# Layer 0's linear attention: its inputs asked for behind the attention keys, state sums one cycle ahead, gate and norm in one step, output weights split in its second pass

## The chip, the cores and the metric

The kernel runs on one core of one Trainium2 chip. The metric is the time of one execution on the device in microseconds (us), the median of several. Five engines work side by side, each through its own queue in order: TensorE (PE: matmuls, with a separate row PEld for the loading of weights), VectorE (DVE), ScalarE (ACT), GpSimd (POOL) and SyncE (SP), whose queue here only issues DMAs. They wait for one another by semaphores.

## What is computed

Two layers over 2048 latent tokens and 256 context tokens, in float32. Layer 0 mixes two branches side by side, a softmax attention over eight heads and a gated linear attention (GLA) over four heads, and a projection with the weight `w_out` joins them. The change lies in layer 0 alone. Its linear part, cut to what matters:

```python
def step(state, inp):
    qi, ki, vi, gi = inp
    b = jnp.cumsum(gi, axis=-2)
    b_last = b[..., -1:, :]
    q_t = qi * jnp.exp(b)
    k_t = ki * jnp.exp(-b)
    att = jnp.where(mask, jnp.einsum('bhld,bhmd->bhlm', q_t, k_t), 0.0)
    o = jnp.einsum('bhld,bhde->bhle', q_t, state) + jnp.einsum('bhlm,bhme->bhle', att, vi)
    k_dec = ki * jnp.exp(b_last - b)
    state = state * jnp.exp(b_last)[..., 0, :, None] + jnp.einsum('bhld,bhle->bhde', k_dec, vi)
    return state, o
...
a = a.reshape(bsz, n, A_WIDTH) * jax.nn.silu(za)
b = rms_norm(b, gla_gain).reshape(bsz, n, B_WIDTH).astype(zb.dtype) * jax.nn.silu(zb)
return jnp.dot(jnp.concatenate([a, b], axis=-1), w_out)
```

The scan runs once forward and once backward over the tokens, and the two outputs are added.

## The kernel before

Tokens are cut into 18 tiles of 128 (two of context, sixteen latent). Layer 0 runs in stages: `even_latent` and `even_rest` make queries, keys, values and gates and leave them in HBM; `even_mix` runs the softmax attention with the linear attention woven into it, and then the projection.

**The softmax attention** (`even_attention`, L961) takes four pairs of heads (j), and for each pair five blocks of queries (nb: one of 256 context queries over two key tiles, four of 512 over all 18 key tiles). For a key tile, PE makes scores in ten matmuls (L1121), ACT takes the exponential into a buffer `apt` (seven of them), and DVE adds it to a running sum `acc` (L1128). The products with the values (L1032, the "tails") are held back: when six key tiles are pending, `flush` does four tails in a row. A finished block is ended by `end` and `finish` (L948 to L958): matmuls that sum the denominators over partitions, then ACT, DVE and POOL, and a store. `flush` does the ends that are due ahead of the tails.

**The linear attention** (`gla`, L679) is a Python generator, `side`. It yields the name of a slot that it wants ("before", "after", "middle", "turn", "second", "unit"), and `place` runs its next piece when the attention comes to a slot of that name: "before", "turn", "unit" and "second" lie in a flush ahead of its tails, "after" behind its tails, "middle" between two flushes, when four key tiles are pending. `issue_after` puts the piece's instructions behind the named ones on the same engine, and the attention's next matmul behind the piece's last one. So PE's order is written out by hand: what a piece waits for, the whole of PE waits for. The order of the other queues comes from the tile scheduler, by the order in the program and by readiness in its own model.

In its first pass, one cycle takes two flushes. For token tile c: `decays(c)` makes the decay factors (`mid` and `hs`, matmuls L762 and L766), the scaled queries `gqt` and keys `gkt` (ACT Exp, then DVE L776; one buffer each); behind the same flush's tails `values(c - 1)` multiplies the scores of the tile before with the values (L817), copies them out (L819), and multiplies `gkt` of the tile before with the values (L823, state sums, scaled into `D` by L824); `scan` then carries the forward state on POOL. The next flush turns queries and keys (`turn`), `within` makes the scores. PSUM gives the linear attention, the turns and the denominators two banks in all (tag "gl").

In its second pass, a slot "second" for each tile, in the backward order: `write` turns the finished tile before (L883), `carried` adds queries times state (L857, L858), `squares` sums squares on ACT and takes the power -1/2 on POOL (`rpow`, L207 to L210), `back` carries the backward state (DVE L837 and L838, POOL L839), `gated` scales by the norm on DVE (L875) and multiplies with the gate on POOL (L876). A flush that has an end due takes no "second".

Behind both passes the side splits the projection's weights: 16 units of 128x512 (`load_unit` L1228, `split_unit` L1231), each split into a high part (ACT copy) and a rest (DVE subtract, L1235), with one slot "unit" for each, into buffers that the linear attention has left. The unit 15 and the loads of the gate rows come behind the attention. `project_load` and `project_split` read and split the first tile of the result.

**The start of the stage.** `want = next(side)` at L1024 runs the head of `gla` before the attention's first loads are traced: loads of `gate_w` (97 partitions), `tri`, `halves`, `gla_norm`, and the inputs of the first tiles (`glr`, `gu`), all on SP's queue. The buffer `ge` that takes `gate_w` lies where the weights of the stage before lay, so that its load waits for that stage's last matmuls. `gw` is made from it: a copy on ACT, a DMA of its own last row, and a subtraction on DVE. Behind that head come the attention's loads (L973 for keys `akh`, `akl` and queries `aq`; L1001 for values). Each DMA takes the next of eight semaphores in turn, and waits until the DMA that had it last has landed.

## Time and profile before

| | us |
|---|---|
| median of 3 runs | 3635.44 |
| lowest and highest | 3629.82, 3636.42 |
| the profiled execution, its time | 3634.33 |
| its span, from the first to the last instruction | 3632.5 |
| PE busy in the span | 3489.4 |
| DVE, ACT, POOL busy | 2346.1, 1391.7, 1344.5 |
| mean granted TensorE clock | 0.985 |

In the rows of the trace a line gives the start, the duration, the engine (SPq is a DMA issue on SP's queue), the line of the kernel, the operation and "out<-in" by the program's names; in brackets stands how long the engine was idle before it, and what ended that. A table of stretches gives the busy time of each engine, the instructions in it in brackets, the granted clock of PE (1.00 is full speed), the busy share of the 16 DMA engines, and GB/s. A row of waits gives the waiting engine and line, what it waited for, and the sum, the number and the longest of these waits. A row of groups gives busy time and mean duration in ns, and behind the bar the idle time before the group's instructions.

### The profile page before, as it was taken

How to read it: one execution, taken by the hardware profiler on the slowest of the kernel's cores; microseconds unless marked ns; L12 is line 12 of the kernel's file. 1: busy time of each engine (PE TensorE's matmuls, PEld its weight loads, DVE VectorE, ACT ScalarE, POOL GpSimd, SP SyncE). 2: the span in 40 equal slices, each digit the busy share in tenths (PEclk: the TensorE clock that was granted, in tenths of full speed). 3: DMA queues.
4: the chain of work that ended last, by engine and by line, in shares of the span. 5: the costliest groups of instructions: out<-in, count | busy, mean ns of one | idle time of the engine just before them, and what ended most of it. 6: DMA issues, size and time to landing. Idle time of an engine off the chain costs nothing. (4 is left out here: it accounts for less than half of the span.)

```text
span 3632.5 us, 53914 instructions
## 1 busy us (share of the span) xinstructions
PE 3489.4 (96%) x19604; PEld 2693.3 (74%) x19604; DVE 2346.1 (65%) x4567; ACT 1391.7 (38%) x2516; POOL 1344.5 (37%) x1430
## 2 busy tenths in 40 slices
PE   7999989999998999999999999999899999999899
PEld 6888988888884666565556888888788887555577
DVE  4677656888884777767766335555578784666732
ACT  5444552111114545445654114444422222555510
POOL 1433430100101344433321234333444443888763
PEclk9999999999999999999999999999999999999999
DMA  7555554222214242334435544555744447888672
GB/s 250 146 158 156 140 153 133 84 69 83 76 61 133 71 126 72 104 103 121 146 97 165 178 136 128 157 160 154 237 128 139 137 132 186 216 225 213 188 235 99
DMA packets 375787, 517.06 MB, mean 142 GB/s; under 512 B 33993, under 2 KB 253593, under 8 KB 369618
## 3 DMA queue, kind: packets, MB, share of 16 engines
q1 hardware_dynamic: 330754, 422.36, 40.3%
q0 software_dynamic: 22112, 63.26, 5.7%
q10 hardware_dynamic: 22656, 27.99, 2.2%
q8 instruction: 156, 2.56, 0.3%
q14 instruction: 109, 0.89, 0.1%
HBM read 334.17 MB, written 179.30 MB: 141 GB/s over the span
## 5 line engine op out<-in xcount | busy, mean ns | idle before, releaser
L661 DVE TENSOR_REDUCE mm<-mx 128x1 f32<-128x512 f32 (+1 forms) x656 | 388.6, 629 | 82.2 <-PE mx L660 75.2
L1128 DVE TENSOR_TENSOR acc<-acc,apt 128x1024 f32<-128x1024 f32 x256 | 362.9, 1417 | 85.2 <-ACT apt L106 66.7
L106 ACT ACTIVATE apt<-st 128x1024 f32<-128x1024 f32 (+1 forms) x296 | 300.3, 1015 | 237.2 <-PE st L1121 217.2
L1121 PE MATMUL st<-aq,akh 64*128 64x512 f32 x1728 | 312.2, 410 | 2.7 <-ACT apt L106 2.5
L1032 PE MATMUL av<-apt,av 128*64 128x512 f32 x1152 | 263.2, 598 | 0.0
L1603 POOL TENSOR_TENSOR oacc<-oacc,opt 128x576 f32<-128x576 f32 (+5 forms) x192 | 223.4, 1189 | 41.0 <-ACT rl L106 19.9
L660 PE MATMUL mx<-mk,mq 96*128 96x512 f32 (+1 forms) x656 | 236.0, 373 | 0.8 <-DMA mq<-QC 0.4
L1721 DVE TENSOR_TENSOR opt<-st,tab 128x64 f32<-128x64 f32 (+10 forms) x576 | 144.5, 318 | 140.6 <-PE st L1564 68.2
L1121 PE MATMUL st<-aq,akl 64*128 64x512 f32 (+1 forms) x1152 | 230.0, 392 | 0.0
L1121 PEld LDWEIGHTS st<-aq,akh 64*128 64x128 f32 x1728 | 151.0, 186 | 86.6 <-ACT apt L106 30.1
L106 ACT ACTIVATE u<-gm 128x352 f32<-128x352 f32 (+1 forms) x140 | 68.5, 497 | 368.6 <-PE gm L131 208.5
L1480 DVE CUSTOM_DVE_ANT_1 mx<-mx,mtab 128x217 f32<-128x217 f32 (+12 forms) x576 | 184.0, 338 | 38.9 <-PE mx L1474 29.8
L1032 PEld LDWEIGHTS av<-apt,av 128*64 128x64 f32 x1152 | 77.7, 137 | 139.4 <-issue 135.7
L106 ACT ACTIVATE opt<-opt 128x930 f32<-128x930 f32 (+7 forms) x129 | 104.2, 810 | 110.8 <-DVE opt L1721 104.0
L660 PEld LDWEIGHTS mx<-mk,mq 96*128 96x128 f32 x656 | 121.2, 188 | 13.5 <-DVE mm L661 1.6
L1121 PEld LDWEIGHTS st<-aq,akl 64*128 64x128 f32 (+1 forms) x1152 | 110.4, 185 | 24.4 <-DMA akl<-KC 0.3
L129 PE MATMUL gm<-w1h,hhi 128*128 128x512 f32 x288 | 116.3, 404 | 7.3 <-ACT onat L106 7.3
L106 ACT ACTIVATE x<-px,modB,modA 128x128 f32<-128x128 f32 x272 | 99.5, 468 | 61.0 <-PE px L339 49.6
L129 PE MATMUL gm<-w0h,hhi 128*128 128x512 f32 x288 | 115.4, 401 | 2.1 <-DVE hhi L351 2.1
L210 POOL TENSOR_TENSOR oss<-oss,mhalf 128x8 f32<-128x8 f32 x68 | 113.2, 1665 | 5.1
L130 PE MATMUL gm<-w1l,hhi 128*128 128x512 f32 x288 | 114.9, 399 | 0.0
L131 PE MATMUL gm<-w1h,hlo 128*128 128x512 f32 x288 | 114.2, 397 | 0.0
(505 smaller groups left out, 9782.4 us busy)
## 6 DMA issues: line engine op xcount, KB each, us to landing
q<-Q SPq DMA_DIRECT2D x48, 512.0 KB
H<-x ACTq DMA_DIRECT2D x36, 512.0 KB
adaw<-ada_w SPq DMA_DIRECT2D x64, 256.0 KB
x<-H SPq DMA_DIRECT2D x32, 512.0 KB
wraw<-w_od SPq DMA_DIRECT2D x64, 256.0 KB
K1t<-okt POOLq DMA_DIRECT2D x32, 512.0 KB, 7.5
kt<-K1t SPq DMA_DIRECT2D x32, 512.0 KB
mtab<-rpb_q SPq DMA_DIRECT2D x16, 899.0 KB
```

The source lines that it names most:

```text
L106: return self.nc.scalar.activation(out, in_, func, **kw)
L129: self.nc.tensor.matmul(out, lh(k), rh(k), start=j == 0, stop=False)
L130: self.nc.tensor.matmul(out, lh(k), rl(k), start=False, stop=False)
L131: yield self.nc.tensor.matmul(out, ll(k), rh(k), start=False, stop=j == n - 1)
L660: mm = nc.tensor.matmul(ps[:, :w], q[:A_QK, (t % 6) * P : (t % 6) * P + P], k[:A_QK, k0 : k0 + w], start=True, stop=True)
L661: nc.vector.tensor_reduce(out=m[:, t, n : n + 1], in_=ps[:, :w], axis=AX.X, op=ALU.max)
L1032: mm = nc.tensor.matmul(O[j, nb][i * 64 : i * 64 + 64, :w], V[j, kt // TT][:, kt % TT, i * 64 : i * 64 + 64], pts[:, i, :w], start=n == 0, ...
L1121: mm = nc.tensor.matmul(ps[:, o // 64, :w], k[o : o + r, kb, kq], Q[o : o + r, qb, :w], start=m == 0, stop=m == 4)
L1128: added = nc.vector.tensor_tensor(out=acc[:, :, :w], in0=a[:, :, :w], in1=pts[:, :, :w], op=ALU.add)
L1480: nc.vector.tensor_tensor_reduce(out=s, in0=s, in1=tb[:, ri : ri + rn, ci : ci + cn], scale=1.0, scalar=-3e38, op0=ALU.add, op1=ALU.max, a ...
L1603: self.psum = nc.gpsimd.tensor_tensor(out=a, in0=a, in1=pts[:, :, a0 - r0 : a1 - r0, :], op=ALU.add)
L1721: bias = nc.vector.tensor_tensor(out=pt[:, d[0], d[1]], in0=ps[:, d[0], d[1]], in1=tabs[j][i][:, ri : ri + rn, ci : ci + cn], op=ALU.add)
```

## The change

- `want = next(side)` moves from L1024 into the pair j = 0, behind all loads of keys, rests and values. The head's ACT copy into `gw` becomes a DVE copy, and `gw`'s three steps move behind `low_rank(1)`.
- `values(c - 1)` keeps the product with the scores; the state sums become `added(c)`, one cycle ahead, in the same slot: they use the keys that `decays(c)` has made in the same flush. `scan` moves with them.
- `flush` does the due ends behind the first tail instead of ahead of all tails.
- In the second pass `carried` comes ahead of `write`; POOL's part of `back` is put behind `rpow`; `gated` is four DVE instructions of 128x128 (multiply by the norm's column, then by the gate) in place of one DVE and one POOL instruction of 128x512.
- `spare(n)` at the end of each slot of the second pass loads and splits units of the output weights, 13 of them by its count; two more follow in slots "unit", then the load and the split of the projection's first tile, from j = 3, nb = 2 on (before: a load at j = 3, nb = 4 and the split at its half).

```diff
@@ -207,7 +207,7 @@
         g = self.nc.gpsimd
         g.tensor_scalar(out=out, in0=in_, scalar1=mul, scalar2=add, op0=ALU.mult, op1=ALU.add)
         shp = list(out.shape)
-        g.tensor_tensor(out=out, in0=out, in1=self.mhalf[:, : shp[1]], op=ALU.pow)
+        return g.tensor_tensor(out=out, in0=out, in1=self.mhalf[:, : shp[1]], op=ALU.pow)
     def consts(self, es):
@@ -676,7 +676,7 @@
         return list(range(NCT - 1, -1, -1)) + list(range(NT - 1, NCT - 1, -1))
-    def gla(self, gp, gs, g1, gd, pp, tag):
+    def gla(self, gp, gs, g1, gd, pp, tag, spare):
         nc = self.nc
         g = nc.gpsimd
@@ -686,9 +686,6 @@
         raw = self.tl(gs, [P, 512], "ge")
         nc.sync.dma_start(raw[:97], self.i["gate_w"])
         gw = self.tl(g1, [98, 512], "gw", F32R, bufs=1)
-        self.act(gw[:97], raw[:97])
-        nc.sync.dma_start(gw[97:98].bitcast(F32), gw[96:97].bitcast(F32))
-        nc.vector.tensor_tensor(out=gw[64:97], in0=raw[64:97], in1=gw[64:97], op=ALU.subtract)
         tri = self.tl(g1, [P, 4, P], "tri", bufs=1)
         nc.sync.dma_start(tri[:], self.i["tri"])
         ind = self.tl(gp, [P, 2], "ind")
@@ -810,19 +807,23 @@
         def values(c):
-            gv, f, _, kt = tiles.pop(c)
-            at = scores.pop(c)
+            gv, at = tiles.pop(c)[0], scores.pop(c)
             ps = bank()
             for h in range(H):
-                nc.tensor.matmul(ps[:, h * P : h * P + P], at[:, h, :], gv[:, h * P : h * P + P], start=True, stop=True)
+                self.woven = nc.tensor.matmul(ps[:, h * P : h * P + P], at[:, h, :], gv[:, h * P : h * P + P], start=True, stop=True)
             oi = self.tl(gs, [P, 512], "goi")
             nc.vector.tensor_copy(oi[:], ps[:])
             nc.sync.dma_start(self.gO[c], oi[:])
+
+        def added(c):
+
+            gv, f, _, kt = tiles[c]
             ps = bank()
             for h in range(H):
                 self.woven = nc.tensor.matmul(ps[:, h * P : h * P + P], kt[:, h * P : h * P + P], gv[:, h * P : h * P + P], start=True, stop=True)
             nc.vector.tensor_tensor(out=Dl[c][:], in0=ps[:].rearrange("p (h t) -> p h t", h=H),
                                     in1=f[:, :, 1:2].to_broadcast([P, H, P]), op=ALU.mult)
+            scan(c, slice(0, 64), g, g, "gsf")
         state = {}
@@ -865,15 +866,14 @@
             for h in range(H):
                 hs = slice(h * P, h * P + P)
                 self.act(sq[:, hs], oi[:, hs], AF.Square, accum_out=ss[:, h : h + 1])
-            self.rpow(ss[:], ss[:], 1.0 / 128, EPS)
-            rows[c] += (ss,)
+            rows[c] += (ss, self.rpow(ss[:], ss[:], 1.0 / 128, EPS))
         def gated(c):
-            _, oi, zb, ss = rows[c]
-            o3 = oi[:].rearrange("p (h t) -> p h t", h=H)
-            nc.vector.tensor_tensor(out=o3, in0=o3, in1=ss[:].unsqueeze(2).to_broadcast([P, H, P]), op=ALU.mult)
-            g.tensor_tensor(out=oi[:], in0=oi[:], in1=zb, op=ALU.mult)
+            _, oi, zb, ss, _ = rows[c]
+            for h in range(H):
+                hs = slice(h * P, h * P + P)
+                nc.vector.scalar_tensor_tensor(out=oi[:, hs], in0=oi[:, hs], scalar=ss[:, h : h + 1], in1=zb[:, hs], op0=ALU.mult, op1=ALU.mult)
         def write(c):
@@ -893,6 +893,9 @@
         yield "after"
         low_rank(0)
         low_rank(1)
+        nc.vector.tensor_copy(gw[:97], raw[:97])
+        nc.sync.dma_start(gw[97:98].bitcast(F32), gw[96:97].bitcast(F32))
+        nc.vector.tensor_tensor(out=gw[64:97], in0=raw[64:97], in1=gw[64:97], op=ALU.subtract)
         yield "after"
         logits(0)
         low_rank(2)
@@ -909,10 +912,12 @@
                 yield "before"
                 decays(c)
                 softplus(c + 1)
+            yield "after"
             if c:
-                yield "after"
                 values(c - 1)
-                scan(c - 1, slice(0, 64), g, g, "gsf")
+            if c < NT:
+                added(c)
+            if c:
                 inputs(c + 1)
             if c < NT:
                 yield "turn"
@@ -927,16 +932,19 @@
         reads(order[0])
         for n in range(NT + 1):
             yield "second"
+            if n < NT:
+                carried(order[n])
             if n:
                 write(order[n - 1])
             if n < NT:
-                carried(order[n])
                 if n + 1 < NT:
                     reads(order[n + 1])
                 squares(order[n])
                 if n + 1 < NT:
-                    back(order[n + 1])
+                    with self.tc.issue_after(rows[order[n]][4].ins):
+                        back(order[n + 1])
                 gated(order[n])
+            spare(n)
     def finish(self, av, dacc, zt, dst, w, ap, pp, tag, lnp=None, bufs=(1, 2), out=None):
@@ -958,7 +966,7 @@
         (out or nc.sync).dma_start(dst, rc[:, :w])
         return rc
-    def even_attention(self, ap, pp, ahead, side):
+    def even_attention(self, ap, pp, side):
         nc = self.nc
         blocks = [(0, CTX, [0, 1])] + [(CTX + 512 * b, 512, list(range(NT))) for b in range(4)]
@@ -1021,7 +1029,7 @@
             return q, last
         pend, late, O, sums = [], [], {}, {}
-        want = next(side)
+        want = None
         def tail(j, nb, n, kt, pts):
@@ -1063,15 +1071,15 @@
             with ExitStack() as es:
                 for x in marks:
                     es.enter_context(self.tc.issue_after(x.ins))
-                for x in due:
-                    with self.tc.issue_after(mm.ins):
-                        mm = end(*x[1:])
-                    late.remove(x)
                 short = None
                 for n in range(5):
-                    if n == 4 and not (short and short[1] not in sums):
-                        break
-                    if not pend:
+                    if n == 1 or not pend:
+                        for x in due:
+                            with self.tc.issue_after(mm.ins):
+                                mm = end(*x[1:])
+                            late.remove(x)
+                        due = []
+                    if not pend or n == 4 and not (short and short[1] not in sums):
                         break
                     p = pend.pop(0)
                     with self.tc.issue_after(mm.ins):
@@ -1097,6 +1105,7 @@
                     next(g)
                 for p in (1, 2):
                     load(keys(0, p), low(0, p), values(0, p))
+                want = next(side)
             else:
                 load(low(j, 2), values(j, 1), values(j, 2))
             for nb, (q0, w, kts) in enumerate(blocks):
@@ -1128,8 +1137,6 @@
                         added = nc.vector.tensor_tensor(out=acc[:, :, :w], in0=a[:, :, :w], in1=pts[:, :, :w], op=ALU.add)
                     if added:
                         marks.append(added)
-                    if (j, nb, n) == (3, 4, NT // 2):
-                        ahead()
                     if n == len(kts) - 1 and nb:
                         sums[j, nb] = [acc[:, i, :w] for i in range(2)]
                     pend.append((j, nb, n, kt, pts))
@@ -1167,40 +1174,53 @@
                 g1 = self.pool(es, "glA", bufs=2, side="right", reuse_waits="tile")
                 pre, w = {}, {}
+                places = [(g1, t) for t in ("gqt", "gkt", "gkT", "gat", "tri")] + [(gd, f"D{c}") for c in self.back_order()]
+                raw = []
+
+                def unit(place=None):
+
+                    u = len(w)
+                    if raw:
+                        if u < 2:
+                            x = self.tl(g1, [P, 1024], "gu", F32R)
+                            place = x[:, :512], x[:, 512:1024]
+                        elif u < 13:
+                            place = [self.tl(q, [P, 512], t, F32R, bufs=1)[:] for q, t in places[2 * u - 4 : 2 * u - 2]]
+                        else:
+                            place = [self.tl(pre["ld"], [P, 512], "wo" + z, F32R)[:] for z in "hl"]
+                        self.split_unit(w, u, raw.pop(), place)
+                        u += 1
+                    if u < 2 * KD - 1:
+                        raw.append(self.load_unit(u, self.tl(g1, [P, 512], "gG", bufs=2)))
+
+                def spare(n):
+
+                    if n > max(len(w), 2 * len(w) - 8) and len(w) < 13:
+                        unit()
+
                 def side():
                     with ExitStack() as esg:
                         gp = self.pool(esg, "glC", side="right", reuse_waits="tile")
                         gs = self.pool(esg, "glS", bufs=2, side="right", reuse_waits="tile")
-                        yield from self.gla(gp, gs, g1, gd, pp, "gl")
+                        yield from self.gla(gp, gs, g1, gd, pp, "gl", spare)
                     ld = pre["ld"] = self.pool(es, "woX", bufs=2, side="right", reuse_waits="tile")
-                    places = [(g1, t) for t in ("gqt", "gkt", "gkT", "gat", "tri")] + [(gd, f"D{c}") for c in self.back_order()]
-                    waiting = []
-                    for u in range(2 * KD):
-                        if waiting:
-                            self.split_unit(w, *waiting.pop())
-                        if u < 2 * KD - 1:
-                            if u < 2:
-                                x = self.tl(g1, [P, 1024], "gu", F32R)
-                                place = x[:, :512], x[:, 512:1024]
-                            elif u < 13:
-                                place = [self.tl(q, [P, 512], t, F32R, bufs=1)[:] for q, t in places[2 * u - 4 : 2 * u - 2]]
-                            else:
-                                place = [self.tl(ld, [P, 512], "wo" + z, F32R)[:] for z in "hl"]
-                            waiting.append((u, self.load_unit(u, self.tl(g1, [P, 512], "gG", bufs=2)), place))
-                            yield "unit"
-
-                def split():
-
-                    ld = pre["ld"]
+                    while len(w) < 2 * KD - 1:
+                        yield "unit"
+                        unit()
+                    while "last" not in pre:
+                        yield "unit"
+                    pre[0] = self.project_load(self.RT, 0, self.i["xin"], ld)
+                    yield "unit"
+                    yield "unit"
                     r, x = pre[0]
                     hi, lo = self.tl(ld, [P, KD, P], "prh", F32R, bufs=1), self.tl(ld, [P, KD, P], "px", F32R)
                     self.project_split(r[:], hi[:], lo[:])
                     pre[0] = hi, lo, r, x
-                for n, _ in enumerate(self.even_attention(ap, pp, split, side())):
-                    if n == 19:
-                        pre[0] = self.project_load(self.RT, 0, self.i["xin"], pre["ld"])
+                for n, _ in enumerate(self.even_attention(ap, pp, side())):
+                    if n == 17:
+                        pre["last"] = True
             sp = self.pool(es, "woS", bufs=2, side="right", reuse_waits="tile")
             pp = self.pool(es, "woP", bufs=2, space=PSUM, reuse_waits="tile")
             self.prep_pool(e1, "prp1", "left", 2, 3)
```

## The prediction

> **What bounds the kernel now.** I read the page first: PE is busy for all but some 4% of the span, and the chain that ended last is PE's.
>
> ```profile
> span 3632.5 us, 53914 instructions
> PE 3489.4 (96%) x19604; PEld 2693.3 (74%) x19604; DVE 2346.1 (65%) x4567; ACT 1391.7 (38%) x2516; POOL 1344.5 (37%) x1430
> ```
>
> A faster DVE or POOL instruction is therefore worth only what PE waits for it. So I asked for PE's waits in the stage that the change touches (1098 to 1950 us), and behind it:
>
> ```profile
> PE st L1121 <- DMA akl<-KC: 16.1, 1, 16.1
> PE gl L823 <- DVE goi L819: 13.3, 17, 0.8
> PE gl L883 <- POOL goi L876: 10.7, 12, 1.2
> PE gl L948 <- ACT gqT L106: 4.7, 8, 0.6
> ...
> PE pj L129 <- ACT D L106: 3.0, 2, 2.0
> ...
> PE pj L129 <- ACT woh L106: 1.0, 1, 1.0
> ```
>
> Each of these is something that a part of the change handles. PE's order is fixed by hand here, so a wait removed moves all that follows, unless PE stops again at the next hand-over.
>
> **Part 1: inputs asked for behind the keys.** The order of time, and PE's clock in stretches:
>
> ```profile
> 1078.59 0.43 SPq L973 DMA_DIRECT2D akl<-KC  x1
> 1099.08 0.24 SPq L687 DMA_DIRECT2D ge<-gate_w  x1
> ...
> 1110.07 0.63 ACT L106 ACTIVATE gw<-ge 97x512 fp32r<-97x512 f32 x1 [8.81 <-issue]
> ...
> 1111.43 0.25 POOL L715 COPY gu<-glr 128x96 f32<-128x96 f32 x1
> ...
> 1113.40 0.42 SPq L973 DMA_DIRECT2D akl<-KC  x1
> ...
> 1117.66 0.55 PE L1121 MATMUL st<-aqc,akl 33*128 33x256 f32 x1 [16.06 <-DMA akl<-KC]
> ...
> 1136.12 0.38 SPq L1001 DMA_DIRECT2D av<-Vn  x1
> ...
> 1138.27 0.42 PE L723 MATMUL gl<-ident,gu 128*96 128x128 f32 x2
> ...
> 1117.60:1125.90 8.30, 8.24 (x51) 6.11 (x51) 1.75 (x2) 4.28 (x5) 0.00 (x0) 0.75 0.66 194
> 1929.90:1934.90 5.00, 5.00 (x42) 3.62 (x40) 2.34 (x2) 3.01 (x3) 0.00 (x0) 1.00 0.18 56
> ```
>
> SP had issued the first `akl` piece at 1078.59 and then stood for 20 us at `gate_w`; the second piece, which PE needs for its first scores, went out at 1113.40, behind the whole head with `gw`'s way through ACT and a DMA. With the head behind the keys it goes out at about 1079. The buffers of all first keys and values start below those of the weights in use until 1099, so I expect the wait to go whole: **-16.1**. PE then also does not come back at the lower clock (0.75 on the mean in that stretch): 51 matmuls, 40 of them full scores, took 8.30 us, where 40 took 5.0 later; the 11 short ones have half the columns, 11 x 0.0625 = 0.7; so **-2.6**.
>
> What is late next is the linear attention's head. The j = 0 loads took from 1113.40 to 1136.5, 23 us; from 1079 they end at 1102, so `gate_w` goes out at about 1102 in place of 1099, and the first copy of `glr`, 12.3 us behind it now (1099.08 to 1111.43), comes at about 1114.5. PE wants it at 1138.27 less 18.7, at 1119.6. That leaves 5 us: no wait, term 0. `gw`'s copy costs DVE 0.7 once (as L819 below), and its subtraction waits there for the landing of `gw`'s last row, with the next sums of `acc` queued behind it; these have buffers, and PE wants `gw` a flush later. [...]
>
> **Part 2: state sums a cycle ahead.** One cycle's hand-over:
>
> ```profile
> 1302.63 0.60 ACT L106 ACTIVATE gkt<-gl 128x512 f32<-128x512 f32 x1 [5.64 <-PE gl L823]
> ...
> 1319.99 0.59 ACT L106 ACTIVATE gqt<-gl 128x512 f32<-128x512 f32 x1
> 1320.29 3.65 PE L1032 MATMUL av<-apt,av 128*64 128x512 f32 x16
> ...
> 1320.99 0.41 ACT L106 ACTIVATE fac<-gl 64x8 f32<-64x8 f32 x3
> ...
> 1322.26 1.76 DVE L776 TENSOR_TENSOR gqt<-gqt,gu 128x512 f32<-128x512 f32 x1
> ...
> 1323.88 1.16 PE L817 MATMUL gl<-gu,gat 128*128 128x128 f32 x8
> ...
> 1325.07 0.69 DVE L819 COPY goi<-gl 128x512 f32<-128x512 f32 x1 [1.05 <-PE gl L817]
> 1325.82 0.38 PE L823 MATMUL gl<-gu,gkt 128*128 128x128 f32 x1 [0.78 <-DVE goi L819]
> ```
>
> ACT's exponential into `gkt` waits for L823 of the tile before, because there is one `gkt`; until then it holds the bank of `mid`. So L817 and L823 share the one free bank, and L823 waits for DVE's copy between them, 0.78 us in 17 cycles. With the sums ahead `gkt` is free, the bank too: **-13.3**. But now PE needs `gkt` of the same flush: ACT can write it by 1321.4 + 0.6 = 1322.0, DVE is done with `gqt` at 1324.02, and with `gkt` 0.07 + 0.69 (the copy's duration) later, at 1324.8; PE is through L817's eight matmuls at 1323.88 + 1.16 = 1325.04, and could issue the next a little before, while the last one drains. It is a tie. I take 0.1 a cycle, **+1.7**; the bounds are 0, and one sum of `acc` (1.42, row below) ahead of it on DVE in 18 cycles, 25.6.
>
> **Part 3: gate and norm in one step, `carried` first, ends behind a tail.**
>
> ```profile
> 1668.42 1.06 PE L857 MATMUL gl<-D,gqT 128*128 128x128 f32 x8
> ...
> 1672.57 1.04 POOL L839 TENSOR_TENSOR D<-gsb,fac 64x512 f32<-64x512 f32 x1 [4.70 <-DVE gsb L838]
> ...
> 1673.98 1.01 POOL L210 TENSOR_TENSOR gss<-gss,mhalf 128x4 f32<-128x4 f32 x1
> ...
> 1675.02 0.69 DVE L875 TENSOR_TENSOR goi<-goi,gss 128x512 f32<-128x512 f32 x1 [2.60 <-POOL gss L210]
> ...
> 1675.85 2.16 POOL L876 TENSOR_TENSOR goi<-goi,gsf 128x512 f32<-128x512 f32 x1 [0.86 <-PE st L1121]
> ...
> 1678.06 1.08 PE L948 MATMUL gl<-acc,mtwos 128*64 128x512 f32 x4
> ...
> L737 DVE SCALAR_TENSOR_TENSOR ge<-gG,gl 128x512 f32<-128x512 f32 x18 | 12.4, 687 | 0.6
> L954 DVE SCALAR_TENSOR_TENSOR gl<-rl,gl 128x256 f32<-128x256 f32 x4 | 1.7, 429 | 0.1
> ```
>
> POOL's product ends at 1678.01, and PE comes to the next flush at 1678.06; where that flush has a slot "second", L883 stands there. Of the 128x128 form the trace has none; from 512 and 256 columns (687 and 429 ns) half the step down again gives 0.30 us, four give 1.2. So `gated` ends some 1.2 us after 1675.0 at the latest, 2 us before PE comes, and `carried` ahead gives another 1.06: **-10.7**. The lower bound for four is 0.69 (one of 512), the upper 4 x 0.43 = 1.7: neither reaches PE. [...]
>
> The ends wait for ACT to empty a turn's bank, 8 times 0.6. One tail of 16/4 matmuls is 3.65/4 = 0.9 us: **-4.7**.
>
> DVE's own load in the two passes (its busy time is the third figure behind the length):
>
> ```profile
> 1140.00:1640.00 500.00, 480.75 (x3364) 301.53 (x3361) 361.67 (x365) 244.70 (x352) 190.63 (x133) 1.00 0.31 95
> 1640.00:1890.00 250.00, 238.72 (x1591) 137.03 (x1591) 184.50 (x179) 146.84 (x324) 86.19 (x79) 1.00 0.40 120
> ...
> L1128 DVE TENSOR_TENSOR acc<-acc,apt 128x1024 f32<-128x1024 f32 x84 | 119.3, 1420 | 14.9 <-ACT apt L106 8.4
> L875 DVE TENSOR_TENSOR goi<-goi,gss 128x512 f32<-128x512 f32 x18 | 12.5, 692 | 44.3 <-POOL gss L210 44.3
> ```
>
> In the second it is busy for 184.5 of 250 us, and stands 44.3 more for `rpow`. Added: 18 x (1.2 - 0.69) = 9.2 for `gated`, 13 x 0.69 = 8.9 for the units. `rpow` ahead of `back` takes 18 x 1.04 = 18.7 from the standing. That makes 184.5 + 18.1 + 25.6 = 228 in 250 - 11 = 239: it fits, at 95%, without ease. I set **+2** for single late sums.
>
> **Part 4: output weights split early.** The projection's start, 62 instructions against 61 a little later:
>
> ```profile
> 1945.50:1970.05 24.55, 19.46 (x62) 13.06 (x61) 12.35 (x16) 9.84 (x15) 2.57 (x2) 0.79 0.77 235
> 1970.05:1983.65 13.60, 13.60 (x61) 11.26 (x61) 9.37 (x14) 7.08 (x11) 2.22 (x2) 1.00 0.67 213
> ```
>
> 24.55 - 62/61 x 13.60 = 10.7 us are lost to late units and, behind these waits, to the clock (0.79). With 15 units split by then only unit 15 is left, which PE needs as the 45th of these matmuls, 10 us in. **-10.7**, and **+1** for that unit. The splits' ACT copies lie in ACT's idle time, which in the second pass is 250 - 146.8 us.
>
> **The sum.** -16.1 - 2.6 - 13.3 + 1.7 - 10.7 - 4.7 + 2 - 10.7 + 1 = -53.4. I give back 1.4 for hand-overs that I have not seen: **-52** from the profiled execution's 3634.3 (span 3632.5 and 1.8 around it; 1.1 under the median shown): **3582**. Its own range is 3574 to 3592.
>
> **The rivals.**
> - DVE is behind by one sum at each `added`: the tie of part 2 is lost, 25.6 in place of 1.7, **3606**. For it: two sums stood ahead of `gqt` in the cycle shown. Against it: these belong to key tiles whose exponentials were done; the next ones cannot be ready before the tails end.
> - The second pass becomes DVE's: with sums pushed into the next slot PE waits in L883 as now, and the standing for `rpow` does not shrink: 184.5 + 18.1 + 44.3 = 247 us, 8 more than PE's 239, so +8 in place of +2 and +10.7 for nothing gained: **3599**. For it: the 95%.
> - The change does not do what it says at the start: another wait, for a buffer or a landing, holds the scores as long; 18.7 are not gained: **3601**. Against it: SP shows nothing to wait for between 1078.59 and 1099.08 but `gate_w`.
> - It comes out slower: `added` in the flush of its own `decays` stands behind DVE's queue. Without part 2 the gain is 52 + 1.7 = 53.7 us, so from a wait of 3.0 us in each of 18 cycles on nothing is left; three sums ahead of `gkt` (4.3 us) give 76.7 and **3657**. Against it: DVE is idle for 138 of 500 us in the first pass.
>
> **Chances.** Forecast 0.64, first rival 0.12, second 0.10, third 0.08, slower 0.04, something that leaves it within 0.2% (what a measurement of this kernel can tell from no change) 0.02. Faster is the sum of the first four, 0.94. The low end, 3570, is all six gains whole (58.1, 3576) and 6 us more, a tenth, for what I have sized too small. The high end, 3610, takes in the first three rivals.
>
> **What would show it.** Right: no wait of PE at `akl<-KC` and a clock of 1.00 at 1105 to 1125; L823 without `goi` as its releaser; L883 out of the waits; splits of L1235 from some 1600 us on, none of the D buffers behind the attention. Wrong: L823 waiting for `gkt` L776 for over 0.5 us a cycle; `st` L1121 waiting for `apt` behind late sums; the first L723 waiting for `glr`; `gate_w` still ahead of the keys on SP.

## The result, and the profile after

The changed kernel took **3571.93 us** (median of 4 runs, 3570.77 to 3578.97) where the kernel before, run beside it, took 3635.93: a ratio of 0.9827, 95% interval 0.9806 to 0.9849, or 64.0 us less. That is faster by 1.7%. The prediction was 3582: the direction and the mechanisms hold, and the time is some 10 us below the forecast (64.0 us gained where 52 were forecast), 2 us outside the likeliest case's own range (3574 to 3592) and inside the full one (3570 to 3610).

The page of the changed kernel, first its busy times:

```profile
PE 3477.3 (97%) x19604; PEld 2691.7 (75%) x19604; DVE 2342.4 (65%) x4622; ACT 1388.7 (39%) x2515; POOL 1277.5 (36%) x1412
```

PE does the same 19604 matmuls in 12.1 us less busy time; POOL is rid of the gate's products. Next PE's waits from 1096 to 1910 us, the stage that was changed:

```profile
PE st L1130 <- DVE u L626: 1.5, 1, 1.5
PE gl L730 <- DVE rT L723: 1.1, 1, 1.1
PE gl L759 <- DVE ge L802: 1.1, 1, 1.1
PE st L1130 <- ACT apt L106: 0.7, 2, 0.6
PE gl L1040 <- ACT gqT L106: 0.6, 1, 0.6
PE pj L130 <- DVE gG L1255: 0.2, 1, 0.2
```

This is the whole list. The waits for `akl`, for `goi` in both places and for the ends' `gqT` (8 times) are gone. New are L730's and one of a tail (L1040), which takes a bank of the linear attention that ACT has yet to empty. Of the waits for units 0.2 us are left, in the last row.

To see where the time came from, the same marks are set in both traces: the last matmul of the stage before (L131), the first tail, the first `carried`, the last tail, and the 62nd matmul of the projection. What lies between the first and the last of these is called "the stretch" from here on. Stretches of the kernel before; the columns are the window, its length, then the busy time and count of PE, PEld, DVE, ACT and POOL, PE's clock, the DMA share and GB/s. The row before the last is the whole stretch, the last what follows it:

```profile
1098.89:1125.95 27.06, 9.54 (x62) 6.76 (x60) 3.17 (x4) 6.79 (x8) 3.26 (x9) 0.68 0.47 143
1125.95:1645.45 519.50, 500.25 (x3497) 313.04 (x3496) 374.40 (x381) 253.73 (x362) 192.96 (x135) 1.00 0.33 100
1645.45:1944.18 298.73, 285.49 (x1869) 160.34 (x1869) 213.16 (x207) 171.92 (x353) 85.15 (x78) 0.99 0.38 112
1944.18:1970.34 26.16, 21.07 (x69) 13.56 (x66) 13.06 (x18) 9.84 (x15) 2.57 (x2) 0.80 0.75 225
1098.89:1970.34 871.45, 816.35 (x5491) 493.70 (x5490) 603.80 (x607) 442.29 (x738) 283.95 (x224) 0.98 0.36 109
1970.34:3632.50 1662.16, 1619.80 (x8340) 1260.04 (x8338) 951.64 (x2575) 595.06 (x1007) 820.69 (x770) 0.99 0.59 171
```

And between the same marks of the changed kernel:

```profile
1096.64:1106.70 10.06, 8.48 (x62) 6.07 (x60) 1.97 (x3) 6.12 (x7) 2.52 (x6) 0.83 0.78 219
1106.70:1606.31 499.61, 496.74 (x3499) 314.24 (x3497) 366.50 (x383) 251.55 (x362) 161.90 (x138) 1.00 0.33 100
1606.31:1890.61 284.30, 283.48 (x1869) 159.16 (x1869) 227.94 (x270) 176.90 (x361) 54.23 (x60) 1.00 0.42 124
1890.61:1906.81 16.20, 15.93 (x70) 11.77 (x66) 6.80 (x8) 5.16 (x8) 2.58 (x2) 1.00 0.50 175
1096.64:1906.81 810.17, 804.63 (x5492) 491.23 (x5490) 603.20 (x662) 439.73 (x738) 221.22 (x206) 1.00 0.37 112
1906.81:3577.20 1670.39, 1620.07 (x8340) 1260.39 (x8338) 948.62 (x2576) 594.32 (x1007) 818.19 (x770) 0.99 0.59 171
```

The stretch is 61.3 us shorter: PE's idle time in it falls from 55.1 to 5.5 (-49.6), and its busy time for the same matmuls by 11.7. This second part the prediction saw only at the start and the end of the stage. What follows is not part of the change; it was 8.2 us longer in this execution, which is the slowest of the four, and 1.6 longer in the repeat below.

The start, in order of time, and PE's clock there:

```profile
1085.00 0.91 SPq L981 DMA_DIRECT2D akl<-KC  x2
...
1098.49 0.50 PE L1130 MATMUL st<-aqc,akh 64*128 64x256 f32 x4 [1.46 <-DVE u L626]
...
1098.77 0.35 SPq L687 DMA_DIRECT2D ge<-gate_w  x1
```

```profile
1100.00:1102.00 2.00, 1.94 (x10) 1.56 (x12) 0.00 (x0) 0.58 (x2) 0.00 (x0) 0.56 1.06 262
1102.00:1104.00 2.00, 2.00 (x14) 1.59 (x12) 0.00 (x0) 1.02 (x1) 0.00 (x0) 0.58 0.43 129
```

The keys are asked for ahead of `gate_w`, and PE's scores start without them missing. In this execution the clock still falls to about 0.57 for some 4 us behind a pause of only 1.46 us; some 1.7 us are lost by it. In the repeat below the same pause of 1.46 us stands there, and the clock stays at 1.00.

One hand-over of the first pass:

```profile
1298.29 1.76 DVE L773 TENSOR_TENSOR gqt<-gqt,gu 128x512 f32<-128x512 f32 x1
...
1299.90 1.16 PE L813 MATMUL gl<-gu,gat 128*128 128x128 f32 x8
...
1299.97 0.68 DVE L773 TENSOR_TENSOR gkt<-gkt,gu 128x512 f32<-128x512 f32 x1
...
1300.94 1.13 PE L823 MATMUL gl<-gu,gkt 128*128 128x128 f32 x8
```

`gkt` is done at 1300.65, and L823 starts at 1300.94 behind its predecessor, without a wait. The margin is 0.29 us here, and between 0.26 and 0.41 us in 14 of the 18 cycles.

DVE in the second pass: its groups from 1600 to 1850 us, then the gate and norm by its tile (the shortest, the median and the longest duration in ns), then one slot:

```profile
L1137 DVE TENSOR_TENSOR acc<-acc,apt 128x1024 f32<-128x1024 f32 x89 | 112.6, 1265 | 16.6 <-ACT apt L106 9.5
L876 DVE SCALAR_TENSOR_TENSOR goi<-goi,gss,gsf 128x128 f32<-128x128 f32 x72 | 35.6, 552 | 22.5 <-POOL gss L210 22.5
```

```profile
L876 DVE SCALAR_TENSOR_TENSOR goi<-goi,gss,gsf x72: 334/340/1243, 1612.4 to 1833.7; 128x128 f32<-128x128 f32 x72
```

```profile
1652.46 2.03 DVE L876 SCALAR_TENSOR_TENSOR goi<-goi,gss,gsf 128x128 f32<-128x128 f32 x4 [0.91 <-POOL gss L210]
1652.50 1.05 POOL L840 TENSOR_TENSOR D<-gsb,fac 64x512 f32<-64x512 f32 x1
...
1657.27 0.60 PE L883 MATMUL gl<-ident,goi 128*128 128x128 f32 x4
```

Four pieces end at 1654.49, and PE comes for them at 1657.27. They take 2.03 us. The first of the four stands beside POOL's product into `D`, which the same `rpow` has let go: in 17 slots it takes 1234 to 1243 ns where the others take 340. In the last slot, which has no such product, the first takes 351 ns and all four 1.14 us.

### The profile page after: what moved, and what is told of

Read it like the earlier page. It is cut to its first block, busy times and chain, and to the rows that moved or that the text cites. A ratio compares the mean times of both kernels' runs of the same rounds, so it can differ in the third digit from the quotient of the medians.

```text
span 3577.2 us, 53986 instructions
## 1 busy us (share of the span) xinstructions
PE 3477.3 (97%) x19604; PEld 2691.7 (75%) x19604; DVE 2342.4 (65%) x4622; ACT 1388.7 (39%) x2515; POOL 1277.5 (36%) x1412
## 4 chain that ended last, share of the span: by engine, by line
PE 83%; DMA 6%; DVE 4%; ACT 2%; POOL 2%; issue 2%; SPq 0%; DVEq 0%; ACTq 0%; POOLq 0%
PE gm L129 10%; PE st L1130 10%; PE gm L130 10%; PE gm L131 10%; PE av L1040 7%; PE mx L660 4%; PE st L1583 2%; PE o L1617 2%; DMA wraw<-w_od 2%; PE pj L130 2%; PE pj L129 2%; PE pj L131 2%; PE st L129 2%; PE st L131 2%; PE st L130 2%
## 5 line engine op out<-in xcount | busy, mean ns | idle before, releaser
L1137 DVE TENSOR_TENSOR acc<-acc,apt 128x1024 f32<-128x1024 f32 x256 | 340.7, 1331 | 79.7 <-ACT apt L106 60.9
L1040 PE MATMUL av<-apt,av 128*64 128x512 f32 x1152 | 265.8, 598 | 0.0
L1500 DVE CUSTOM_DVE_ANT_1 mx<-mx,mtab 128x217 f32<-128x217 f32 (+12 forms) x576 | 183.8, 338 | 37.6 <-PE mx L1494 28.3
L1040 PEld LDWEIGHTS av<-apt,av 128*64 128x64 f32 x1152 | 76.3, 136 | 135.2 <-issue 134.3
L130 PE MATMUL gm<-w0l,hhi 128*128 128x512 f32 x288 | 114.2, 397 | 0.0
```

What stands on the lines that cost most here:

```text
L130: self.nc.tensor.matmul(out, lh(k), rl(k), start=False, stop=False)
L1040: mm = nc.tensor.matmul(O[j, nb][i * 64 : i * 64 + 64, :w], V[j, kt // TT][:, kt % TT, i * 64 : i * 64 + 64], pts[:, i, :w], start=n == 0, ...
L1137: added = nc.vector.tensor_tensor(out=acc[:, :, :w], in0=a[:, :, :w], in1=pts[:, :, :w], op=ALU.add)
L1500: nc.vector.tensor_tensor_reduce(out=s, in0=s, in1=tb[:, ri : ri + rn, ci : ci + cn], scale=1.0, scalar=-3e38, op0=ALU.add, op1=ALU.max, a ...
```

## The experiments

Each kernel was timed beside the kernel before; "gain" is the difference of the two medians, the stretch that of the profiled execution. The intervals reach some 6 us to either side, so smaller differences are read from the traces.

| kernel | median, us | ratio (95% interval) | gain, us | stretch, us |
|---|---|---|---|---|
| changed kernel, repeated | 3574.83 | 0.9835 (0.9819 to 0.9851) | 59.2 | 811.3 |
| head ahead of the keys | 3596.4 | 0.9899 (0.9879 to 0.9919) | 37.6 | 833.3 |
| `gw` made in the head | 3574.28 | 0.9834 (0.9817 to 0.9851) | 59.7 | 812.2 |
| before, with two `gkt` | 3614.05 | 0.9945 (0.9929 to 0.996) | 19.9 | 849.8 |
| gate on POOL | 3576.46 | 0.9842 (0.9827 to 0.9857) | 56.3 | 815.4 |
| `write` first | 3582.66 | 0.9862 (0.9844 to 0.9879) | 50.1 | 820.0 |
| ends first | 3579.87 | 0.9849 (0.983 to 0.9868) | 52.9 | 819.4 |
| no early units | 3586.37 | 0.9869 (0.9853 to 0.9884) | 46.4 | 820.5 |
| `gkt` 2 us later | 3614.18 | 0.9951 (0.9936 to 0.9966) | 18.3 | 856.0 |
| gate in eight pieces | 3579.45 | 0.9851 (0.9836 to 0.9867) | 53.0 | 815.2 |
| `gw`'s row asked for by ACT | 3578.4 | 0.9851 (0.9836 to 0.9866) | 54.1 | 814.8 |
| `gw`'s row loaded | 3570.38 | 0.9824 (0.9811 to 0.9838) | 62.8 | 809.1 |

**The changed kernel once more**, unedited, to see whether the 8 us behind the stretch belong to it.

> The changed kernel once more, for its own scatter. Theory: all of the gain arises between the last matmul of the stage before and the 62nd matmul of the projection; in the first profile of the changed kernel that stretch was shorter by 61.3 us, and the 8 us that it lost again in layer 1 belong to that execution. Then this execution shows the same stretch within 1 us, layer 1 is within 3 us of that of the kernel before, and the ratio is 0.982 to 0.984. Rival: the new order of the program costs layer 1 some 8 us in every execution; then the profile again shows the projection's end to the program's end 8 us longer than before.

Its stretch, and what follows it:

```profile
1098.72:1910.01 811.29, 804.34 (x5492) 491.43 (x5490) 603.63 (x662) 439.81 (x738) 221.56 (x206) 1.00 0.37 112
1910.01:3573.80 1663.79, 1619.39 (x8340) 1260.20 (x8338) 946.94 (x2576) 594.75 (x1007) 816.50 (x770) 0.99 0.59 171
```

The stretch repeats within 1.1 us, and the rest is 1663.79: the 1670.39 belonged to one execution. The variants below are held against this repeat.

**The head ahead of the keys** (part 1's order undone, the rest kept):

```diff
-        want = None
+        want = next(side)
...
-                want = next(side)
```

> The changed kernel with the head of the linear attention in front of the keys again, but gw's three steps still behind low_rank(1). Theory: what held the keys was the head's loads as such: the third load of glr waits for the first one, which lands behind gate_w some 11 us after its issue, so PE waits again for akl, 13 to 16 us, then runs at the lower clock, and the time is 15 to 19 us above the changed kernel. Rival: it was gw's way through ACT and a second DMA; without it the keys go out right behind the head's ten issues, some 5 us after 1099, and PE waits 5 to 8 us only.

SP's and POOL's rows at the start (the last row is PE's wait for the second `akl` piece):

```profile
1111.47 0.47 POOL L712 COPY gu<-glr 128x96 f32<-128x96 f32 x2
1111.75 0.32 SPq L710 DMA_DIRECT2D glr<-Un  x1
1112.12 0.42 SPq L981 DMA_DIRECT2D akl<-KC  x1
...
1114.09 0.55 PE L1129 MATMUL st<-aqc,akl 33*128 33x256 f32 x1 [13.03 <-DMA akl<-KC]
```

The wait is back with 13.0 us, though `gw`'s three steps are no longer in the head. The third load of `glr` stood for the buffer of the first one, which POOL's copy, from 1111.47 on, gave free behind the landing of `gate_w`; the keys stood behind it on SP. So the position of the head is the cause, and `gw`'s steps were not what held it. A wait of 5.9 us in L730 comes on top. Theory right, the price (21.6 us of gain) a little above what it named.

**`gw` made in the head**, on ACT, as before:

```diff
+        self.act(gw[:97], raw[:97])
+        nc.sync.dma_start(gw[97:98].bitcast(F32), gw[96:97].bitcast(F32))
+        nc.vector.tensor_tensor(out=gw[64:97], in0=raw[64:97], in1=gw[64:97], op=ALU.subtract)
...
-        nc.vector.tensor_copy(gw[:97], raw[:97])
-        nc.sync.dma_start(gw[97:98].bitcast(F32), gw[96:97].bitcast(F32))
-        nc.vector.tensor_tensor(out=gw[64:97], in0=raw[64:97], in1=gw[64:97], op=ALU.subtract)
```

> The changed kernel with gw's three steps (ACT copy, DMA, subtraction) in the head again, the head itself behind the keys. Theory (the position of the head is what counts): ACT's copy stands ahead of the fourth exponential of the block of 512 and waits there for gate_w, which lands at about 1110, so ACT stops for 3 to 6 us and PE, which has two score buffers, waits 2 to 5 us: 2 to 6 us above the changed kernel. Rival: with the keys loaded first gw's steps cost nothing: within 1 us.

ACT stands for `gate_w`, and PE waits 3.8 us for its exponentials; but `gw` is then early and L730 does not wait. Gain and stretch are the repeat's within 1 us. The mechanism that the theory named is seen, no net price of it.

**The kernel before with two `gkt`**, its sums where they were (one unit of the output weights then goes into the second buffer; those lines of the edit are left out here):

```diff
-            kt = self.tl(g1, [P, 512], "gkt", bufs=1)
+            kt = self.tl(g1, [P, 512], "gkt", bufs=2)
```

> The kernel before with a second buffer of gkt and nothing else of the change (one unit of weights goes to the second buffer). Theory: L823 waits only because the one gkt keeps ACT's exponential, and with it the bank of mid, until L823 is done; with two buffers L823 starts 0.99 us behind L817's first matmul as in the changed kernel (1.94 before), in 17 cycles, so 16 us below the kernel before, and the sums need not go a cycle ahead. Rival: the two products take the same bank one after the other whatever gkt does; then 1.94 us stays and the time is that of the kernel before within 3 us.

One hand-over, and the first pass (first tail to first `carried`):

```profile
1317.56 1.16 PE L817 MATMUL gl<-gu,gat 128*128 128x128 f32 x8
...
1318.56 1.06 PE L823 MATMUL gl<-gu,gkt 128*128 128x128 f32 x8
```

```profile
1124.95:1626.61 501.66, 495.72 (x3498) 311.50 (x3496) 374.47 (x381) 251.55 (x362) 167.67 (x135) 1.00 0.33 104
```

The wait of L823 is gone without a sum being moved, and L823 stands 1.00 us behind L817 where it stood 1.94 behind. So the cause of the wait was the one that the prediction named: one `gkt` held the bank of `mid`. The row also sizes the term: against the kernel before, PE's idle time in this pass falls from 19.25 to 5.94, by 13.3 as predicted, **and its busy time falls by another 4.5**. The whole is 17.8. It lies in two places: from L817's last matmul to L823's first 18.10 us become 2.01, and the steps within L823's matmuls 15.80 us become 14.07.

**The gate on POOL again** (part 3's one step undone, its order kept):

```diff
-            for h in range(H):
-                hs = slice(h * P, h * P + P)
-                nc.vector.scalar_tensor_tensor(...)
+            o3 = oi[:].rearrange("p (h t) -> p h t", h=H)
+            nc.vector.tensor_tensor(out=o3, in0=o3, in1=ss[:].unsqueeze(2).to_broadcast([P, H, P]), op=ALU.mult)
+            g.tensor_tensor(out=oi[:], in0=oi[:], in1=zb, op=ALU.mult)
```

> The changed kernel with gated as before (one DVE product of 128x512 by the norm, one POOL product by the gate). Theory: POOL's 2.0 us at the end of the chain is what L883 waited for; with rpow ahead of back and carried ahead of write 2.1 us of the chain are saved already, so of the 10.7 us of waits at most 2 come back: 0 to 4 us above the changed kernel. Rival: the one step is what counts, L883 waits for POOL in 12 slots again, 8 to 12 us above.

The pair of DVE and POOL instructions that `rpow` lets go, in one slot:

```profile
1665.47 0.69 DVE L875 TENSOR_TENSOR goi<-goi,gss 128x512 f32<-128x512 f32 x1 [0.91 <-POOL gss L210]
1665.52 1.55 POOL L840 TENSOR_TENSOR D<-gsb,fac 64x512 f32<-64x512 f32 x1
```

L883 waits for POOL's product 6 times, 2.3 us in all, where it was 10.7 us before the change. The one-step gate is worth 2.9 us by the gains and 4.1 by the stretch; most of part 3's gain is thus made without it. That it is made by `rpow` ahead of `back` and `carried` ahead of `write` is likely, but no kernel has `rpow` alone put back.

**`write` ahead of `carried` again**:

```diff
-            if n < NT:
-                carried(order[n])
             if n:
                 write(order[n - 1])
             if n < NT:
+                carried(order[n])
```

> The changed kernel with write ahead of carried again. Theory: gated ends 2 us before PE comes to the slot, so the order of the two does not matter: no wait in L883 and within 1 us of the changed kernel. Rival: PE waits for DVE's last gated, some 0.5 to 1 us in 12 slots, 6 to 12 us above.

One slot in order of time:

```profile
1708.41 0.69 DVE L859 TENSOR_TENSOR goi<-gl,goi 128x512 f32<-128x512 f32 x1
...
1709.20 0.31 ACT L106 ACTIVATE ge<-goi 128x128 f32<-128x128 f32 x1 [3.56 <-DVE goi L859]
...
1710.39 1.91 ACT L106 ACTIVATE apt<-st 128x1024 f32<-128x1024 f32 x2
...
1711.44 0.73 PE L1129 MATMUL st<-aq,akh 64*128 64x512 f32 x4 [0.89 <-ACT apt L106]
```

PE waits 6.7 us for `apt`, in 6 places like the last row, and not once in L883. `carried`'s sums reach DVE a little later, its addition L859 ends late, ACT's squares stand for that addition, and the next exponential stands behind the squares on ACT, for which PE waits. The price is 9.1 us of gain, of which the second pass has 7.4 (291.48 us against the repeat's 284.10). Its size is the rival's, its way neither's: the order of these two steps guards ACT's queue.

**The ends ahead of the tails again**:

```diff
-                    if n == 1 or not pend:
+                    if n == 0 or not pend:
```

> The changed kernel with the due ends ahead of all tails again. Theory: the denominators wait for ACT to empty a turn's bank, 8 times 0.6 us and some 0.15 of drain each, 5 to 6 us above the changed kernel. Rival: ACT, which no longer stands for L823, empties the bank sooner, and nothing comes back.

The wait for `gqT` returns (L956, 4.7 us in 8 times), and the first pass grows by 7.6 us. The theory's size is met, but not by its terms. Two periods of this pass are at half the clock, one of twice 3.41 us from L730's wait on and one of 3.41 us behind a pause of 1.05 us at L759:

```profile
1128.87:1135.70 6.83, 6.27 (x28) 4.63 (x30) 6.07 (x8) 1.68 (x2) 0.45 (x1) 0.50 0.02 4
1524.82:1528.23 3.41, 3.41 (x9) 0.99 (x10) 1.25 (x2) 1.21 (x5) 2.37 (x4) 0.50 0.76 254
```

The repeat has one period of 3.41 us in this pass, behind L730, so that 3.1 us of the 7.6 come from the clock, at places where the edit changed nothing. L730's wait is 0.4 longer. What is left for the ends is 4.1 us, and that is idle time alone: their 4.7, less the 0.6 that the tail L1040 no longer waits.

**No early units**: all units in slots "unit" as before (in `spare`, the condition is made false).

```diff
-                    if n > max(len(w), 2 * len(w) - 8) and len(w) < 13:
+                    if False:
```

> The changed kernel without the splits in the second pass: all units behind it, one to a slot. Theory: the units still left at the end of the attention are split late, the projection's first 62 matmuls take 23 to 25 us again in place of 14.8, and the time is 9 to 12 us above the changed kernel; DVE, freed of 13 subtractions in the second pass, gives nothing back there because PE did not wait for it. Rival: the second pass gains 3 us or more, so that only 5 to 8 us remain.

From the last tail to the 62nd matmul the projection takes 22.8 us in place of 16.3, PE waits 3.2 us for ACT's parts of units in `D`, and the second pass is 3.3 us longer. 12.8 us of gain are lost by the medians and 9.2 by the stretch, where the prediction gave 9.7 for part 4. The second pass did not gain what the rival named, nor stay as it was, as the theory had it.

**`gkt` later by 2 us**: three copies of `gkt` onto itself ahead of its product on DVE. The output stays the same.

```diff
                 self.act(dst[:], mid[:], AF.Exp, scale=sc)
+                for _ in range(3 if dst is kt else 0):
+                    nc.vector.tensor_copy(kt[:], kt[:])
```

> The changed kernel with three more DVE copies of gkt onto itself (128x512) between ACT's exponential and the product that L823 needs. In the changed kernel gkt is ready 0.26 to 0.41 us before L823 starts in 14 of 17 cycles. Theory: that margin is all there is; three copies of some 0.4 us make PE wait 0.9 to 1.1 us in these cycles, 13 to 16 us, and with what a wait costs beside its idle time 14 to 22 us above the changed kernel. Rival: DVE's order leaves more room (the copies take the place of idle time ahead of gkt), and less than 6 us come.

PE's wait, and the first pass:

```profile
PE gl L825 <- DVE gkt L775: 26.2, 15, 2.0
```

```profile
1101.15:1647.34 546.19, 514.01 (x3499) 325.64 (x3497) 397.63 (x437) 251.41 (x362) 157.90 (x138) 0.97 0.29 92
```

The copies took 0.69 us each, 2.06 in a cycle, and PE waited 1.7 us in 15 cycles: the margin of 0.3 is all there is, and DVE is on PE's path behind it. The pass is 43.8 us longer than the repeat's 502.4 for 27.9 us more of idle time. The other 15.9 lie in PE's busy time, at a clock of 0.97 on the mean: nine periods of 3.41 us at half the clock, where the repeat has one, make some 13.6 of them. The theory's way is met, its 14 to 22 us are not (40.9 of gain): it gave a copy 0.4 us, and too little to the clock.

**The gate in eight pieces** of 128x64:

```diff
-            for h in range(H):
-                hs = slice(h * P, h * P + P)
+            for i in range(8):
+                h, hs = i // 2, slice(i * 64, i * 64 + 64)
```

> The changed kernel with gated in eight DVE instructions of 128x64 in place of four of 128x128. In the changed kernel the four take 2.0 us together (0.55 each on the mean, beside POOL's work) and PE waits for apt only 0.16 and 0.58 us in the second pass. Theory: the second pass is at DVE's limit; another 1 to 1.5 us in each of 18 slots makes DVE late, ACT's squares stand in front of the exponentials, and PE waits for apt: 8 to 18 us above the changed kernel, with waits of L1130 for apt over 5 us. Rival: DVE takes it up in the flushes that end a block: within 3 us.

Eight pieces take 2.54 us of a slot in place of 2.03, and PE waits 5.3 us for `apt` in 5 places; 6.2 us of gain are lost by the medians, 3.9 by the stretch. DVE's 9.3 us more in the pass (44.9 against 35.6 for these pieces) thus cost PE about half of themselves: DVE has room for some of it, not for all. The price lies between the theory's and the rival's, and the extra work, 0.51 us in a slot, is less than the 1 to 1.5 us that the theory named.

**`gw`'s row asked for by ACT**, so that it does not stand behind SP's loads of queries:

```diff
-        nc.sync.dma_start(gw[97:98].bitcast(F32), gw[96:97].bitcast(F32))
+        nc.scalar.dma_start(gw[97:98].bitcast(F32), gw[96:97].bitcast(F32))
```

> The changed kernel with the DMA of gw's last row issued from ACT's queue in place of SP's. Theory: DVE stands 8.2 us for that row because its issue lies behind a block's query loads on SP (copy done at 1118.8, issue at 1125.96, landed at 1128.1); from ACT it lands some 2 us behind the copy, DVE stands under 3 us, L730 no longer waits for rT, and the dip of the clock behind it goes: stretch 1 to 4 us shorter than the changed kernel's 810 to 811. Rival: it changes nothing but the place of DVE's wait: within 1 us.

```profile
1124.64 0.61 ACTq L897 DMA_DIRECT2D gw<-gw  x1
...
1125.30 1.94 ACT L106 ACTIVATE apt<-st 128x1024 f32<-128x1024 f32 x2 [9.07 <-DMA aqc<-QA]
```

A miss. The issue now stood on ACT for 9.07 us, until SP's load of `aqc`, issued at 1121.93 with the same semaphore, had landed: a DMA of this kernel waits for the one that had its semaphore last, here one of another queue. All exponentials stood behind it, and PE waited 4.8 us. The question it was to answer went to the next kernel.

**`gw`'s row loaded** with `gate_w` itself, so that no DMA lies between copy and subtraction:

```diff
         nc.sync.dma_start(raw[:97], self.i["gate_w"])
+        nc.sync.dma_start(raw[97:98], self.i["gate_w"][96:97])
...
-        nc.vector.tensor_copy(gw[:97], raw[:97])
-        nc.sync.dma_start(gw[97:98].bitcast(F32), gw[96:97].bitcast(F32))
+        nc.vector.tensor_copy(gw[:98], raw[:98])
```

> The changed kernel with gw's last row loaded from gate_w itself (row 96 once more, behind the first load, into row 97 of the raw tile) and rounded by the same copy, so that no DMA stands between the copy and the subtraction on DVE. Theory: in the changed kernel DVE stood 8.2 us for that row, whose DMA was behind SP's loads of aqc, and PE waited 1.1 us (2.8 in the repeat) in L730 for what DVE was late with; with the row there, the 8.2 us go, the wait of L730 goes, and the stretch is 1 to 4 us shorter than the 810 to 811 of the changed kernel, so the median 1 to 4 us under the repeat's 3574.8, which is about the limit of what can be told. Rival: the logits wait for the transposes' copies rT, which are not late for the row; DVE's 8.2 us lay in its idle time, L730 waits as before, and stretch and median stay within 1 us.

The last row's DMA and DVE's subtraction in the changed kernel, then DVE's two rows in this one:

```profile
1125.96 0.58 SPq L897 DMA_DIRECT2D gw<-gw  x1
...
1128.10 0.69 DVE L898 TENSOR_TENSOR gw<-ge,gw 33x512 fp32r<-33x512 f32 x1 [8.23 <-DMA gw<-gw]
```

```profile
1118.58 0.42 DVE L897 CAST gw<-ge 98x512 fp32r<-98x512 f32 x1
1119.04 0.69 DVE L898 TENSOR_TENSOR gw<-ge,gw 33x512 fp32r<-33x512 f32 x1
```

DVE's 8.23 us of standing and L730's wait (1.1 us, and in the repeat 2.5, where the expectation has 2.8) are gone, and the stretch is 1.1 to 2.2 us shorter, as the theory had it. In the median it is the fastest kernel of all, but its interval overlaps the changed kernel's: that it is faster than that one is not shown.

## Why the prediction was right, and where its sizes failed

Its terms against the same marks of the two profiled executions:

| | predicted | measured |
|---|---|---|
| part 1, to the first tail | -16.1 - 2.6 = -18.7 | 10.06 - 27.06 = -17.0 |
| parts 2 and 3, the two passes | -13.3 + 1.7 - 10.7 - 4.7 + 2 = -25.0 | 783.9 - 818.2 = -34.3 |
| part 4, the end | -10.7 + 1 = -9.7 | 16.20 - 26.16 = -10.0 |
| hand-overs not seen | +1.4 | 0 |
| sum | -52 | -61.3 |

**Part 1** is right. All of the wait went, and what is late next was met: the first L720 did not wait. The first copy of `glr` came at 1114.16, where 1114.5 was forecast, but by other steps: `gate_w` went out at 1098.77 in place of 1102, and the copy came 15.4 us behind it, not the 12.3 that the prediction took over from the kernel before. Of the clock's 2.6 us only some 1 was won in this execution, since the clock is halved for 3.41 us behind the pause of 1.46 us ahead of the first scores. That is chance, as far as these runs show: the kernels that ask for the keys first all have this pause, and in 4 of their 11 profiled executions it is followed by such a period. In the repeat it is not, and the start takes 8.51 us: -18.6, the whole of the predicted 18.7. What the prediction said of `gw`'s last row, that DVE stands for it with nothing urgent behind, is not quite so: `rT` is behind it in DVE's order, and L730 waits 1.1 us (2.5 in the repeat). The kernel with the row loaded shows that as the cause.

**Parts 2 and 3** have the right mechanisms and the wrong size; this is the step that failed. The idle times were read rightly: between first and last tail PE's idle time fell from 19.25 + 13.24 = 32.5 to 2.87 + 0.82 = 3.7, by 28.8, where the prediction has 13.3 + 10.7 + 4.7 = 28.7. Two things were missed, which together make the 9.3 us between forecast and result in these two passes:

- **A wait cost more than its idle time.** PE's busy time for the same matmuls fell by 5.5 us (785.7 to 780.2), of which the prediction counted nothing. The kernel before with two `gkt` shows it alone: 13.3 idle and 4.5 busy. The trace counts PE as busy for the 1.16 us of L817, and where L823 doesn't wait it starts 1.00 us behind L817: 0.16 us that overlap are lost with each wait, 17 x 0.16 = 2.7 of the 4.5; the other 1.7 lie within L823's own matmuls. In the second pass 2.0 us of busy time went, and 1.7 of it is one period at half the clock that the kernel before has behind a wait of 1.96 us for `apt`. The ends' waits cost their idle time alone.
- **The two charges to DVE, +1.7 and +2, were not made.** The tie of part 2 was won by 0.3 us in most cycles: `gkt` was ready 0.75 us behind the start of L813, where I had 0.92, and L823 comes 1.04 behind it. In the second pass DVE's addition to `acc` took 1265 ns on the mean in place of 1420, 14 us less for 89 of them, with POOL's products gone from beside it: in the kernel with the gate on POOL the mean is 1540 in the same window. That was not in my sum.

The term of `gated`, 1.2 us, was mis-sized: it takes 2.03. The pieces themselves were sized rightly (1.14 us in the slot without POOL's product); what was missing is POOL beside them. That did no harm, since 2.8 us were left until PE came. As to its fullness, the slots "second", from the first `carried` to the last `write`, are this row:

```profile
1606.31:1837.11 230.80, 229.99 (x1534) 131.90 (x1532) 195.61 (x242) 149.24 (x330) 52.94 (x59) 1.00 0.47 141
```

DVE was busy for 195.6 of 230.8 us and stood 22.5 more for `rpow`, 94%; the prediction had 95%.

**Part 4** is right to 0.3 us: the clock is 1.00 at the end in place of 0.80, and PE's only wait for a unit is 0.2 in place of 1.

**The rivals.** None came about, but the first two were near. A DVE behind by one sum at `added` (1.42 us) is what the kernel with the late `gkt` makes, a little larger, and it costs 41 us of gain where the rival named 25.6; the argument against it, that sums ahead of `gkt` belong to key tiles already done, was right, with a margin of 0.3 us. The second, that the second pass becomes DVE's, begins to come true with half a microsecond more in each slot. The slower case had its price from 3.0 us of wait in a cycle (its 53.7 us are the gain without part 2's charge, not without part 2); as a wait of 1.7 costs 2.7 with the clock, it would start near 2 us, an estimate from the kernel with the late `gkt`.

The two single prices for the first pass, 17.8 (two `gkt`) and 4.1 (ends, without the clock's part), add up to 21.9. The changed kernel won 19.9 there, and its new wait in L730 took 1.1; the repeat won 17.1, and L730 took 2.5 and the half clock behind it 1.7. That makes 21.0 and 21.3, so less than 1 us is not placed. What stays open is which pauses bring the half clock, and the single share of `rpow` ahead of `back`.

## What to carry to other kernels

Where PE's order is fixed by hand, sum the idle times of its waits by stretch, and then look at its busy time for the same matmuls between the same marks: here removed waits were worth 1.0 (the ends) to 1.3 times (L823) their idle time, and the added ones of the late `gkt` about 1.6 times. Before a difference of a few microseconds is put down to an edit, count the periods at half the clock in both traces. When a wait "for a copy" is listed, ask which buffer or bank stands behind it: a second `gkt` alone removes what moving the sums removed, and before a DMA is moved to another queue, see whose semaphore it will wait for.

## What the runs showed of the hardware

**The clock fell behind some short pauses, and not behind others.** The kernel with the late `gkt`, whose 15 waits are 2 us at most, has nine periods of 3.41 us at half the clock in its first pass, 1.7 us lost in each; the changed kernel has one behind 1.46 us. Of that pass's 15 pauses between 1.7 and 2.4 us, six have none, and behind the 1.46 us 7 of 11 executions have none. The nine begin at whole multiples of 3.41 us from one another. Pauses of 1.5 to 2 us, and one of 1.05 us in the kernel with the ends first, thus stood ahead of such a period in some cases; why others of the same length did not, these runs do not show.

**DVE and POOL took longer side by side.** In 17 slots of the changed kernel the first `gated` piece takes some 1240 ns beside POOL's product of 1.05 us, and 351 ns in the slot without it. In the kernel with the gate on POOL, DVE's multiplication is let go at the same moment, takes its usual 0.69, and POOL's product takes 1.55. Of the changed kernel's 256 sums of `acc`, the 196 that no POOL instruction overlaps took 1.22 us on the mean, the 60 others 1.68 (both from the single rows). Let go together, the two take nearly the sum of their single durations, some 0.15 us less: the pair of 0.69 and 1.05 takes 1.60 in all, the pair of 0.35 and 1.05 1.24. Why the longer one is DVE's in the changed kernel and POOL's in the other is not shown: DVE's start is listed 0.04 to 0.05 us ahead of POOL's in both.

**A DMA's semaphore tied two queues together** in this kernel, which takes its semaphores in turn: in the row of 9.07 us on ACT the issue stood for SP's load of `aqc`.
